# The values of the local attention group read stored parts of h instead of making them from x

## Chip, core and metric

The kernel runs on one core of a Trainium2 chip. The metric is the time of one execution in microseconds on the device. Engines are named as in the profile: PE (TensorE, matrix products), DVE (VectorE), ACT (ScalarE), POOL (GpSimd) and SP (SyncE), which here does nothing but issue DMAs.

## What is computed

One decoder layer over 2048 tokens of width 1024, in float32. A modulated input h feeds one wide projection; three groups of four attention heads with windows of different stride and a gated short convolution follow, are merged, projected, and normalised. Cut to what the change touches:

```
shift, scale, gate = split(silu(c) @ w_ada + b_ada)
h = x * (1 + scale) + shift
q, k, v, g_attn, u, b_gate, c_gate, g_conv, m_attn, m_conv = split(h @ W_in)
for group, (window, dilation) in enumerate(((128, 1), (512, 4), (2048, 16))):
    o[group], lse[group] = dilated_attention(q, k, v of its 4 heads)
o = sum(softmax(lse over groups) * o)
a_out = (o * silu(g_attn)) @ w_attn_out
s_out = (b_gate * conv3(c_gate * u) * silu(g_conv)) @ w_conv_out
y = (sigmoid(m_attn) * a_out + sigmoid(m_conv) * s_out) @ w_o
x = layer_norm(alpha * x + (1 + gate) * y) * ln_g + ln_b
```

## The kernel before

Every matrix product is made of three products of rounded parts: an operand is split into a high part (a cast to fp32r on ACT, L523) and a low part (operand minus high part on DVE, L524), and the products high x high, low x high and high x low are summed in PSUM (L140 to L142, L621 to L623). "Parts" below means such a pair.

**First stage, 0 to about 1540 us: h times W_in.** It runs in two passes p over 1024 tokens each. Of every four blocks of a product, a scheme with seven products instead of eight is used; its stationary or moving operands are sums and differences of the blocks of h. They are the tiles T[1..7, i] (`th`, `tl`), made once per pass for the four rows i by `t_row`. Row i covers k-tile i (tile `xa`) and k-tile i + 4 (tile `xb`), each of 128 rows of h by the 1024 tokens of the pass, that is, two chunks of 512. T[1], T[2] and T[3] are the parts of whole blocks of h: the first chunk of k-tile i, the first chunk of k-tile i + 4, and the second chunk of k-tile i + 4. The second chunk of k-tile i (b12) enters in sums only; no tile holds its parts.
In pass 0 the four rows are made while scale and shift are still being computed: `first_h` loads two w_ada tiles of 512 KB for each k-tile (`wt`, five buffers, L795), forms their dot products with silu(c) on DVE (L720) or by a multiplication on POOL and accumulations on ACT (L724, L727), and then `load_h` loads x (L737, 256 KB each) and turns it into h on ACT (L738). In pass 1 only `load_h` and `t_row` run, interleaved with the last products of pass 0. Tiles `big` (xa, xb and results) have four buffers, half tiles `t` seven.

**Second stage, about 1540 to 2430 us: attention.** Groups 1 and 2 run first. The local group 0 follows, in chunks c of 512 tokens: values V of chunk 0, V of chunk 1, output segments of chunk 0, V of chunk 2, output of chunk 1, V of chunk 3, output of chunks 2 and 3. For V, `prep` loads x for eight k-tiles (`xs`, three buffers, L84), scales and shifts it on DVE (L85) and splits it into `hhi` and `hlo`, rings of 13 tiles that are shared with the rows of the convolution's and the attention's outputs (eight and four tiles per chunk, `prep_rows`, L93). The products of a V are matmuls of 128 columns by 256, `mm<-whi,hhi` and its two companions. Between them stand the merging of the groups (tiles `ab`, `og`, `gt`, `om_scr`) and the gating of outputs (`sg`, L325 and L331).

**Third stage:** the product with W_o and the normalisation.

A scheduler fixes the order of the instructions of each engine when the program is built, and waits are semaphores. Each engine works in its order; all DMAs are issued by SP, in SP's order. An engine reaches an instruction only after the one before it has been issued, and a DMA whose data or buffer is not ready holds up all DMAs behind it.

Of the kernel before, what the change touches and what calls it, by code (L numbers as in the profile page):

```python
# [11 lines left out]
F32 = mybir.dt.float32  # L12
F32R = mybir.dt.float32r
# [4 lines left out]
P = 128  # L18
DM = 1024
SEQ = 2048  # L20
KT = DM // P
CH = 512
# [30 lines left out]


def attention_stage(tc, psum1, wp, hp, kq, pa, pm, split, ident, scp, mod, w_v, w_ao, w_co, xm, xn,
                    qk_scr, nb_scr, ga_scr, o_scr, st_scr, st0_scr, al_scr, om_scr, y_scr, sg_scr, mg_scr):
    nc = tc.nc
    V, S, G, PE, SP = nc.vector, nc.scalar, nc.gpsimd, nc.tensor, nc.sync

# [14 lines left out]
    def parts_of(xs, store):  # L74
        hi = hp.tile([P, CH], F32R, name="hhi", bufs=13)
        lo = hp.tile([P, CH], F32R, name="hlo", bufs=13)
        split(hi, lo, xs)
        store.append((hi, lo))

    def prep(src, store):  # L80
        def pre():
            for k in range(KT):
                xs = hp.tile([P, CH], F32, name="xs", bufs=3)
                SP.dma_start(xs, src[:, k, :])  # L84
                V.tensor_scalar(xs, xs, scp[:, k:k + 1], mod[:, 0, k:k + 1], op0=ALU.mult, op1=ALU.add)  # L85
                parts_of(xs, store)
        return pre

    def prep_rows(srcs, store):
# [315 lines left out]
    for c in range(NCH):  # L405
# [64 lines left out]
        v_prev = heads_of(0, c, h, hb, v_prev, st, done)  # L470
        for jj in range(NH):
            after(len(segs) + 3 + jj // 2, lambda jj=jj, merge=merge: merge(jj))
        pre_all(first, xn[c], h, None)
        if c > 0:
            out_segs(c - 1)
    out_segs(NCH - 1)
# [7 lines left out]
def layer_kernel(ctx: ExitStack, tc: tile.TileContext, x, xm, xn, cvec, wada, bada, w_main, w_v,  # L484
# [25 lines left out]
    nb_scr = dram.tile([3, NH, P, 256], F32, name="nb_scr")  # L510
    qk_scr = dram.tile([24, P, SEQ], F32, name="qk_scr")
    ga_scr = dram.tile([NH, P, SEQ], F32, name="ga_scr")
    o_scr = dram.tile([2, NH, NCH, NCH, P, P], F32, name="o_scr")
    st_scr = dram.tile([2, NCH, NH, 4, 2, NCH, 32], F32, name="st_scr")
    st0_scr = dram.tile([NCH, 2, NH * 4, P], F32, name="st0_scr")
# [40 lines left out]
    def half():  # L556
        return rooms["prep"].tile([P, CH], F32, name="t", bufs=7)
# [4 lines left out]
    def t_split(T, p, i, src):  # L562
        hi = rooms[i].tile([P, CH], F32R, name=f"th{p}{i}")
        lo = rooms[i].tile([P, CH], F32R, name=f"tl{p}{i}")
        split(hi, lo, src)
        T[p, i] = (hi, lo)

    def t_row(T, i, xa, xb):

# [129 lines left out]
    def sum_to(dst):  # L699
        return lambda r, bank: V.tensor_add(dst, r, bank)  # L700

    def t_rows(T, loads):

        def pre():
            for i, load in loads:
                xa, xb = big(), big()
                load(xa, xb)
                t_row(T, i, xa, xb)
        return pre


# [68 lines left out]
    with block_products("s", "prep", (0, 1, 2)) as w:  # L780
# [4 lines left out]
        with tc.tile_pool(name="ada", bufs=1, reuse_waits="tile") as ada:  # L785
# [21 lines left out]
                return load  # L807

            S0 = load_parts(w, w_main[W_Q + NH], w_main[W_Q + NH + 1], CH)
            t_rows(T, [(i, first_h(i)) for i in range(3)])()  # L810
            xa, xb = big(), big()
            first_h(3)(xa, xb)
        open_room((3,))
        t_row(T, 3, xa, xb)
        for n in range(KT):
            SP.dma_start(cw[:, n, :3], convw[n])
        SP.dma_start(cw[:, :, 3], convb)
# [12 lines left out]
        for p in range(2):  # L830
            pre = None
            if p:
                T = {}
                pre = t_rows(T, [(i, load_h(p, i)) for i in range(4)])


            order = [u + g * NH + j for g in (1, 2, 0) for u in (W_Q, W_K) for j in (0, 2)]
# [128 lines left out]
    with ExitStack() as stage:  # L966
        psum1 = stage.enter_context(tc.tile_pool(name="psum", bufs=1, space=bass.MemoryType.PSUM,
                                                 reuse_waits="tile"))
        pool = lambda name: stage.enter_context(tc.tile_pool(name=name, bufs=1, reuse_waits="tile"))
        wp, hp, pm, kq, pa = (pool(n) for n in ("wp", "hp", "pm", "kq", "pa"))  # L970
        attention_stage(tc, psum1, wp, hp, kq, pa, pm, split, ident, scp, mod, w_v, w_ao, w_co, xm, xn,
                        qk_scr, nb_scr, ga_scr, o_scr, st_scr, st0_scr, al_scr, om_scr, y_scr, sg_scr, mg_scr)

    w = ctx.enter_context(block_products("s", (1, 2, 3), (0,), "prep"))

# [119 lines left out]
```

## Time and profile before

| | us |
|---|---|
| median of 3 runs | 2683.31 (2682.05 to 2684.86) |
| profiled execution, its own time | 2677.93 |
| its span, first to last instruction | 2676.1 |
| PE busy | 2468.6 (92%) |
| DVE busy | 1727.0 (65%) |
| ACT busy | 1043.8 (39%) |
| POOL busy | 66.4 (2%) |

The DMA queues moved 361.94 MB; 274.32 MB were read from and 85.51 MB written to HBM. The shares are means over stages with different limits, so they are read by stretches: what counts is where PE is idle, and which engine or queue it waits for there.

### The profile page before, as it was taken

To read this page: it belongs to the slowest core of one execution; us is meant where nothing else is said; L and a number is where in the kernel's file an instruction comes from. 1 tells how busy PE (TensorE), PEld (TensorE's weight loads), DVE (VectorE), ACT (ScalarE), POOL (GpSimd) and SP (SyncE) were. 2 spreads that over 40 slices of the span, in tenths; PEclk is the share of its full clock that TensorE was granted. 3 is DMA by queue.
4 is the path that set the end of the run, shared out by engine and by line. 5 is a ranking of instruction groups with operands and counts; after the bars stand their busy time and mean duration, and the time that the engine had idled before them with its cause. 6 is when DMAs were issued, how large, how long until landed. Compare 5 with 4: busy or idle time off the path is not lost. (4 is left out here: it accounts for less than half of the span.)

```text
span 2676.1 us, 31985 instructions
## 1 busy us (share of the span) xinstructions
PE 2468.6 (92%) x11878; PEld 2091.5 (78%) x11878; DVE 1727.0 (65%) x2867; ACT 1043.8 (39%) x1741; POOL 66.4 (2%) x46
## 2 busy tenths in 40 slices
PE   3999999999999999999999989999998797987884
PEld 2778888888876888888888779999997687864663
DVE  8754566767567555666765355455578777667785
ACT  5323333333344223333333355545563334223443
POOL 2000000000000000000000000000000000000222
PEclk8999999999999999999999989999998898988997
DMA  6334322222343332212122274355558878673332
GB/s 236 119 105 146 107 79 71 68 67 103 126 160 130 104 124 97 87 64 71 63 94 97 87 227 146 110 142 150 161 164 242 268 219 280 202 239 118 126 122 90
DMA packets 196552, 361.94 MB, mean 135 GB/s; under 512 B 21629, under 2 KB 92460, under 8 KB 196396
## 3 DMA queue, kind: packets, MB, share of 16 engines
q1 hardware_dynamic: 196396, 359.90, 42.3%
q8 instruction: 93, 1.52, 0.2%
q14 instruction: 63, 0.52, 0.1%
HBM read 274.32 MB, written 85.51 MB: 134 GB/s over the span
## 5 line engine op out<-in xcount | busy, mean ns | idle before, releaser
L621 PE MATMUL pb<-th,w2h 128*128 128x512 f32 x2016 | 798.4, 397 | 81.3 <-ACT th L523 50.2
L622 PE MATMUL pb<-tl,w2h 128*128 128x512 f32 x2016 | 796.9, 396 | 14.0 <-DVE tl L524 13.9
L623 PE MATMUL pb<-th,w2l 128*128 128x512 f32 x2016 | 793.1, 394 | 5.7 <-DVE w2l L524 5.7
L621 PEld LDWEIGHTS pb<-th,w2h 128*128 128x128 f32 x2016 | 383.3, 190 | 179.8 <-ACT th L523 59.8
L622 PEld LDWEIGHTS pb<-tl,w2h 128*128 128x128 f32 x2016 | 383.6, 190 | 104.3 <-DVE tl L524 25.0
L623 PEld LDWEIGHTS pb<-th,w2l 128*128 128x128 f32 x2016 | 383.8, 190 | 88.3 <-DVE w2l L524 8.8
L524 DVE TENSOR_TENSOR w2l<-raw,w2h 128x1024 fp32r<-128x1024 f32 x168 | 214.1, 1275 | 151.0 <-ACT w2h L523 151.0
L523 ACT CAST w2h<-raw 128x1024 fp32r<-128x1024 f32 x168 | 176.8, 1052 | 287.5 <-PE pb L622 271.6
L630 ACT COPY t<-pb 128x512 f32<-128x512 f32 x248 | 144.6, 584 | 351.7 <-PE pb L623 351.7
L140 PE MATMUL mm<-whi,hhi 128*128 128x256 f32 x768 | 251.5, 328 | 18.8 <-ACT hhi L523 18.6
L142 PE MATMUL mm<-whi,hlo 128*128 128x256 f32 x768 | 248.2, 326 | 2.6 <-DVE hlo L524 2.4
L141 PE MATMUL mm<-wlo,hhi 128*128 128x256 f32 x768 | 248.9, 325 | 0.0
L140 PEld LDWEIGHTS mm<-whi,hhi 128*128 128x128 f32 x768 | 185.7, 242 | 21.4 <-ACT hhi L523 20.9
L142 PEld LDWEIGHTS mm<-whi,hlo 128*128 128x128 f32 x768 | 185.0, 242 | 4.2 <-DVE hlo L524 4.1
L141 PEld LDWEIGHTS mm<-wlo,hhi 128*128 128x128 f32 x768 | 186.2, 242 | 0.0
L140 PE MATMUL mm<-hhi,whi 128*128 128x512 f32 x384 | 155.9, 407 | 30.1 <-DVE sg L331 21.3
L523 ACT CAST whi<-raw 128x1024 fp32r<-128x1024 f32 x96 | 100.7, 1050 | 190.3 <-PE mm L141 87.1
L524 DVE TENSOR_TENSOR wlo<-raw,whi 128x1024 fp32r<-128x1024 f32 x96 | 116.9, 1218 | 68.2 <-ACT whi L523 68.1
L141 PE MATMUL mm<-hlo,whi 128*128 128x512 f32 x384 | 153.6, 400 | 0.7 <-DVE hlo L524 0.7
L142 PE MATMUL mm<-hhi,wlo 128*128 128x512 f32 x384 | 153.5, 400 | 0.0
L523 ACT CAST w2h<-xs 128x1024 fp32r<-128x1024 f32 x84 | 88.6, 1055 | 155.2 <-PE pb L622 127.4
L621 PE MATMUL pb<-th,w1h 128*128 128x512 f32 x336 | 131.8, 392 | 3.3 <-DVE big L1013 2.8
(171 smaller groups left out, 3403.6 us busy)
## 6 DMA issues: line engine op xcount, KB each, us to landing
raw<-in_w_main SPq DMA_DIRECT2D x152, 512.0 KB
qk_scr<-big SPq DMA_DIRECT2D x48, 512.0 KB
raw<-in_w_v SPq DMA_DIRECT2D x48, 512.0 KB
sg_scr<-big SPq DMA_DIRECT2D x32, 512.0 KB
sg<-sg_scr SPq DMA_DIRECT2D x64, 256.0 KB
raw<-in_w_co SPq DMA_DIRECT2D x32, 512.0 KB
qr<-qk_scr SPq DMA_DIRECT2D x48, 256.0 KB
ab<-al_scr SPq DMA_DIRECT2D x48, 256.0 KB
```

Of the source, the lines that this page charges most:

```text
L140: PE.matmul(o, a[0], b[0], start=start, stop=False)
L141: PE.matmul(o, a[0], b[1], start=False, stop=False)
L142: PE.matmul(o, a[1], b[0], start=False, stop=stop)
L523: S.copy(hi, src)
L524: V.tensor_sub(lo, src, hi.bitcast(F32))
L621: PE.matmul(bank, a[0], b[0], start=start, stop=False, **kw)
L622: PE.matmul(bank, a[0], b[1], start=False, stop=False, **kw)
L623: PE.matmul(bank, a[1], b[0], start=False, stop=stop, **kw)
L630: S.copy(r, bank)
```

## The change

A DRAM tensor `h_scr` of 16.8 MB takes the parts of all of h (4 chunks, 8 k-tiles, high and low, 128 x 512 each). In the first stage the rows of T store the pairs that T holds (T[1], T[2], T[3]), and `h_rows` makes and stores the parts of b12: one cast, one subtract, two half tiles. That is eight stores of 256 KB per row, eight rows in all. In the local group `prep_split` loads the high and low parts of a chunk straight into `hhi` and `hlo`: sixteen loads of 256 KB per chunk in place of eight loads of x, eight scalings, eight casts and eight subtracts. Groups 1 and 2 still load and scale x.

```diff
+    def prep_split(c, store):
+        def pre():
+            for k in range(KT):
+                hi = hp.tile([P, CH], F32R, name="hhi", bufs=13)
+                lo = hp.tile([P, CH], F32R, name="hlo", bufs=13)
+                SP.dma_start(hi.bitcast(F32), h_scr[c, k, 0])
+                SP.dma_start(lo.bitcast(F32), h_scr[c, k, 1])
+                store.append((hi, lo))
         return pre
...
-        pre_all(first, xn[c], h, None)
+        segs[first][2] = prep_split(c, h)
...
+    h_scr = dram.tile([NCH, KT, 2, P, CH], F32, name="h_scr")
...
+    def h_out(c, k, pair):
+        for n in range(2):
+            SP.dma_start(h_scr[c, k, n], pair[n].bitcast(F32))
+
+    def h_rows(T, p, i, xa):
+
+        hi, lo = half().bitcast(F32R), half().bitcast(F32R)
+        split(hi, lo, xa[:, CH:PAIR])
+        h_out(2 * p + 1, i, (hi, lo))
...
-    def t_rows(T, loads):
+    def t_rows(T, loads, p=None):
 
         def pre():
             for i, load in loads:
                 xa, xb = big(), big()
                 load(xa, xb)
+                if p is not None:
+                    h_rows(T, p, i, xa)
                 t_row(T, i, xa, xb)
+                if p is not None:
+                    for q, c, k in ((1, 0, i), (2, 0, i + 4), (3, 1, i + 4)):
+                        h_out(2 * p + c, k, T[q, i])
         return pre
...
-            t_rows(T, [(i, first_h(i)) for i in range(3)])()
+            t_rows(T, [(i, first_h(i)) for i in range(3)], 0)()
             xa, xb = big(), big()
             first_h(3)(xa, xb)
         open_room((3,))
+        h_rows(T, 0, 3, xa)
         t_row(T, 3, xa, xb)
+        for q, c, k in ((1, 0, 3), (2, 0, 7), (3, 1, 7)):
+            h_out(c, k, T[q, 3])
...
-                pre = t_rows(T, [(i, load_h(p, i)) for i in range(4)])
+                pre = t_rows(T, [(i, load_h(p, i)) for i in range(4)], p)
```

The change also moves instructions. First place: SP's queue at the start, from the fourth w_ada tile of row 2 on. A name such as `tl_410` is one buffer of a tile; `th_381`, `tl_382` to `th_409`, `tl_410` are T[1], T[2], T[3] of row 2, and `t` is a half tile of `h_rows`. Before, loads of w_ada and x alternate:

```order
L795 DMA wt<-in_wada 128x1024 x4
L737 DMA big<-in_xn 128x512 x4
L795 DMA wt<-in_wada 128x1024 x4
L737 DMA big<-in_xn 128x512 x4
L795 DMA wt<-in_wada 128x1024
L816 DMA cw<-in_convw 128x3 x2
L795 DMA wt<-in_wada 128x1024 x3
L737 DMA big<-in_xn 128x512 x4
L816 DMA cw<-in_convw 128x3 x6
```

Now the stores of a row stand between the loads of the next:

```order
L763 DMA big<-in_xn 128x512 x4
L821 DMA wt<-in_wada 128x1024 x3
L581 DMA h_scr<-t 128x512 x2
L581 DMA h_scr<-th_381 128x512
L581 DMA h_scr<-tl_382 128x512
L581 DMA h_scr<-th_385 128x512
L581 DMA h_scr<-tl_386 128x512
L581 DMA h_scr<-th_409 128x512
L581 DMA h_scr<-tl_410 128x512
L821 DMA wt<-in_wada 128x1024
L763 DMA big<-in_xn 128x512 x4
L845 DMA cw<-in_convw 128x3 x8
```

The last w_ada tile and the four x tiles of row 3 (L821, L763 of the new program) moved from a place behind loads only to a place behind the eight stores of row 2. Second place: SP's queue at the change of pass. Before:

```order
L684 DMA raw<-in_w_main 128x1024 x2
L737 DMA big<-in_xn 128x512 x4
L948 DMA sg_scr<-big 128x1024
L737 DMA big<-in_xn 128x512
L948 DMA sg_scr<-big 128x1024
L737 DMA big<-in_xn 128x512 x11
L684 DMA raw<-in_w_main 128x1024 x3
```

Now, with the stores of row 0 of pass 1 ahead of all but one of the tiles of row 1:

```order
L763 DMA big<-in_xn 128x512 x4
L977 DMA sg_scr<-big 128x1024
L763 DMA big<-in_xn 128x512
L977 DMA sg_scr<-big 128x1024
L581 DMA h_scr<-t 128x512 x2
L581 DMA h_scr<-th_5712 128x512
L581 DMA h_scr<-tl_5713 128x512
L581 DMA h_scr<-th_5716 128x512
L581 DMA h_scr<-tl_5717 128x512
L581 DMA h_scr<-th_5740 128x512
L581 DMA h_scr<-tl_5741 128x512
L763 DMA big<-in_xn 128x512 x6
```

Eleven x loads in a row became six behind eight stores, and the rest further down behind the stores of row 1. Third place: V of chunk 2, first on PE, where `hhi_16772` to `hhi_16793` are the first four k-tiles. Before, from the fourth k-tile on:

```order
L140 MATMUL mm_16879<-whi_16825,hhi_16793 128x256
L141 MATMUL mm_16879<-wlo_16826,hhi_16793 128x256
L142 MATMUL mm_16879<-whi_16825,hlo_16794 128x256
L223 MATMUL pt_17315<-ident_60,p_17236 128x128
L223 MATMUL pt_17315<-ident_60,p_17239 128x128 x2
L223 MATMUL pt_17315<-ident_60,p_17249 128x128
L223 MATMUL pt_17324<-ident_60,p_17249 128x128
L223 MATMUL pt_17324<-ident_60,p_17252 128x128 x2
L223 MATMUL pt_17324<-ident_60,p_17236 128x128
L140 MATMUL s_17335<-kh_17144,qh_17143 128x256
```

Now, at the place of the fourth k-tile and after it (`hhi_16830` is the fourth, `hhi_16846` the eighth):

```order
L150 MATMUL mm_16904<-whi_16850,hhi_16830 128x256
L151 MATMUL mm_16904<-wlo_16851,hhi_16830 128x256
L152 MATMUL mm_16904<-whi_16850,hlo_16831 128x256
L150 MATMUL mm_16904<-whi_16854,hhi_16834 128x256
L151 MATMUL mm_16904<-wlo_16855,hhi_16834 128x256
L152 MATMUL mm_16904<-whi_16854,hlo_16835 128x256
L150 MATMUL mm_16904<-whi_16854,hhi_16838 128x256
L151 MATMUL mm_16904<-wlo_16855,hhi_16838 128x256
L152 MATMUL mm_16904<-whi_16854,hlo_16839 128x256
```

The transposes and scores that stood between k-tile 4 and k-tile 5 are gone from there, and the eight k-tiles follow each other. On SP's queue at the same V, before, from the store of o on:

```order
L465 DMA om_scr<-o_16398 128x512
L65 DMA raw<-in_w_v 128x1024
L333 DMA mg_scr<-sg_16729 128x4x128
L333 DMA mg_scr<-sg_16747 128x4x128
L84 DMA xs<-in_xn 128x512 x3
L320 DMA sg_16833<-sg_scr 128x512
L320 DMA sg_16851<-sg_scr 128x512
L65 DMA raw<-in_w_co 128x1024 x2
L84 DMA xs<-in_xn 128x512
```

Now, with the loads of the parts (L94, L95 of the new program):

```order
L475 DMA om_scr<-o_16447 128x512
L94 DMA hhi<-h_scr 128x512
L65 DMA raw<-in_w_v 128x1024
L343 DMA mg_scr<-sg_16778 128x4x128
L343 DMA mg_scr<-sg_16796 128x4x128
L95 DMA hlo<-h_scr 128x512
L94 DMA hhi<-h_scr 128x512
L95 DMA hlo<-h_scr 128x512
L94 DMA hhi<-h_scr 128x512
L95 DMA hlo<-h_scr 128x512
L94 DMA hhi<-h_scr 128x512
L95 DMA hlo<-h_scr 128x512
```

Three more such pairs follow at once, so that seven pairs stand behind the store of o, and one had been loaded earlier; before, four loads of x stood there, and four had been issued some 40 us earlier.

## Rows read from the trace of the kernel before

**Rows 1.** Page, busy time, share of the span, instructions of TensorE:
```profile
PE 2468.6 (92%) x11878; PEld 2091.5 (78%) x11878; DVE 1727.0 (65%) x2867; ACT 1043.8 (39%) x1741; POOL 66.4 (2%) x46
```

**Rows 2.** Busy time by stretch: us, engines (instructions), clock, DMA share, GB/s:
```profile
0.00:50.00 50.00, 16.16 (x39) 10.13 (x40) 42.08 (x112) 25.10 (x56) 11.16 (x12) 0.93 0.68 239
50.00:100.00 50.00, 40.65 (x146) 29.56 (x145) 46.29 (x94) 26.98 (x48) 4.97 (x2) 0.86 0.45 151
...
800.00:850.00 50.00, 44.57 (x175) 32.60 (x175) 41.17 (x60) 29.56 (x44) 0.00 (x0) 0.97 0.36 121
1900.00:1950.00 50.00, 49.66 (x377) 49.42 (x375) 32.88 (x86) 31.68 (x76) 0.00 (x0) 1.00 0.65 186
...
2100.00:2150.00 50.00, 43.52 (x284) 39.68 (x285) 36.39 (x68) 25.12 (x49) 0.00 (x0) 0.90 0.88 285
...
2200.00:2250.00 50.00, 34.88 (x183) 29.81 (x182) 41.72 (x74) 14.88 (x34) 0.00 (x0) 0.83 0.87 267
```

**Rows 3.** Groups by form, 1900 to 2280, DVE, ACT: busy, mean ns, idle before:
```profile
L524 DVE TENSOR_TENSOR hlo<-xs,hhi 128x512 fp32r<-128x512 f32 x64 | 42.3, 687 | 21.2 <-ACT hhi L523 20.7
L85 DVE TENSOR_SCALAR xs<-xs,scp,mod 128x512 f32<-128x512 f32 x24 | 12.6, 540 | 9.2 <-DMA xs<-in_xn 8.9
...
L523 ACT CAST hhi<-xs 128x512 fp32r<-128x512 f32 x64 | 38.1, 618 | 35.5 <-DVE xs L85 13.0 <-DMA xs<-om_scr 9.9 <-DMA xs<-y_scr 7.1
```

**Rows 4.** Timelines of SP, POOL, ACT, DVE, PE at the start: start, us, instruction:
```profile
47.63 2.54 SPq L795 DMA_DIRECT2D wt<-in_wada  x3
...
51.19 2.57 POOL L724 TENSOR_TENSOR wt<-wt,row 128x1024 f32<-128x1024 f32 x1 [10.33 <-DMA wt<-in_wada]
55.55 2.41 POOL L724 TENSOR_TENSOR wt<-wt,row 128x1024 f32<-128x1024 f32 x1 [1.79 <-DMA wt<-in_wada]
...
67.70 1.24 ACT L738 ACTIVATE big<-big,mod,scp 128x1024 f32<-128x1024 f32 x1 [0.28 <-DVE scp L804]
...
53.98 0.68 DVE L574 TENSOR_TENSOR t<-big 128x512 f32<-128x512 f32 x1
...
55.72 2.78 DVE L524 TENSOR_TENSOR tl<-t,th 128x512 fp32r<-128x512 f32 x1
...
66.53 0.69 DVE L574 TENSOR_TENSOR t<-big 128x512 f32<-128x512 f32 x1
...
74.98 0.69 DVE L524 TENSOR_TENSOR tl<-t,th 128x512 fp32r<-128x512 f32 x1
...
79.41 0.50 PE L621 MATMUL pb<-th,w2h 128*128 128x512 f32 x1 [1.55 <-ACT t L630]
```

**Rows 5.** Timelines of SP, ACT and DVE at the change of pass:
```profile
797.84 13.34 SPq L737 DMA_DIRECT2D big<-in_xn  x11
...
801.58 1.24 ACT L738 ACTIVATE big<-big,mod,scp 128x1024 f32<-128x1024 f32 x1 [0.52 <-DMA big<-in_xn]
...
802.86 0.69 DVE L574 TENSOR_TENSOR t<-big 128x512 f32<-128x512 f32 x1 [0.22 <-ACT big L738]
...
823.74 0.68 DVE L524 TENSOR_TENSOR tl<-big,th 128x512 fp32r<-128x512 f32 x1
```

**Rows 6.** Timelines of SP and PE around the values of chunks 2 and 3:
```profile
2105.39 0.32 SPq L465 DMA_DIRECT2D om_scr<-o  x1
...
2110.93 0.28 PE L140 MATMUL mm<-whi,hhi 128*128 128x256 f32 x1
2111.05 0.28 PE L141 MATMUL mm<-wlo,hhi 128*128 128x256 f32 x1
...
2137.82 0.28 PE L142 MATMUL mm<-whi,hlo 128*128 128x256 f32 x1
...
2237.34 0.58 PE L140 MATMUL mm<-whi,hhi 128*128 128x256 f32 x1 [3.54 <-ACT hhi L523]
```

**Rows 7.** Busy time of the 10 us at V of chunk 2, columns as in 2:
```profile
2110.00:2120.00 10.00, 9.52 (x67) 8.39 (x66) 8.13 (x18) 4.41 (x11) 0.00 (x0) 0.98 0.95 318
```

**Rows 8.** Waits of PE in the whole run: us in total, times, longest:
```profile
PE mm L140 <- DVE sg L331: 21.5, 4, 10.5
```

More of the change, by code (lines that the diff above doesn't have):

```diff
@@ L55, in attention_stage @@
 def attention_stage(tc, psum1, wp, hp, kq, pa, pm, split, ident, scp, mod, w_v, w_ao, w_co, xm, xn,
-                    qk_scr, nb_scr, ga_scr, o_scr, st_scr, st0_scr, al_scr, om_scr, y_scr, sg_scr, mg_scr):
+                    qk_scr, nb_scr, ga_scr, o_scr, st_scr, st0_scr, al_scr, om_scr, y_scr, sg_scr, mg_scr, h_scr):
     nc = tc.nc
@@ L86, in pre @@
                 parts_of(xs, store)
+        return pre
+    def prep_split(c, store):
[6 more added lines that the diff above has]
+                store.append((hi, lo))
         return pre
@@ L971, in layer_kernel @@
         attention_stage(tc, psum1, wp, hp, kq, pa, pm, split, ident, scp, mod, w_v, w_ao, w_co, xm, xn,
-                        qk_scr, nb_scr, ga_scr, o_scr, st_scr, st0_scr, al_scr, om_scr, y_scr, sg_scr, mg_scr)
+                        qk_scr, nb_scr, ga_scr, o_scr, st_scr, st0_scr, al_scr, om_scr, y_scr, sg_scr, mg_scr, h_scr)
     w = ctx.enter_context(block_products("s", (1, 2, 3), (0,), "prep"))
```

## The prediction

> **What bounds the kernel now.** I read the page first: TensorE (PE) is busy 2468.6 us of a span of 2676.1 us [rows 1]. So the time falls only where PE is idle, and it grows wherever PE is made to wait; DVE's 1727 us and ACT's 1044 us cost nothing while PE is fed. Then the table of busy time in 50 us stretches [rows 2]: the reader is to see where the idle lies. The first 100 us leave PE 33.8 + 9.4 = 43.2 us idle, the change of pass at 800 to 850 leaves 5.4 us, the values of chunks 0 and 1 (near 1900 to 1950) run under a full PE (49.66 of 50), and the two stretches with the values of chunks 2 and 3 leave 6.5 and 15.1 us. In all four places with idle PE the vector engine or the DMA engines are near full. The durations of single instructions come from the table of instruction groups [rows 3]. Last I read, inside the four places, the timelines of the engines that PE waits for, to see which queue is last [rows 4 to 6]. The change touches exactly these places, so three terms follow: A start-up, B change of pass, C local attention group.
>
> **A, start-up.** It adds per row i of T one cast on ACT, one subtract on DVE and eight stores of 256 KB on SP's queue. DVE is the busiest engine here (42.1 and 46.3 us of the two 50 us stretches, [rows 2]), so four subtracts of 0.69 us [rows 3] are 2.8 us that nothing hides: the lower bound. A gain is excluded, since nothing is taken away here. The casts (0.62 us) lie beside it on ACT, 25 of 50 us busy.
> The larger part is the queue. Before, SP issued the loads of w_ada and x of the next row as soon as a buffer was free; no load there stands behind work on the row before. Now, by the order shown with the change, the last w_ada tile and the four x tiles of row 3 stand behind the store of a tl split of row 2. SP works in order, so those loads can be issued only when DVE has made that split. Step by step, for row 3: before, its last three w_ada loads were issued from 47.63 us on, within 2.54 us, so the last near 49.8; GpSimd (POOL) multiplied the last at 55.55 for 2.41, the last activation of x (L738) ran at 67.70, the first vector step of row 3 at 66.53, its last split began at 74.98, and PE ran without gaps from 79.41 [rows 4]. After: row 2's first vector step, 53.98 before [rows 4], comes some 1.5 us later by the same queueing one row earlier; the split on which the load hangs is the fifth of its steps, 5 x 0.61 plus one step that took 2.78 in place of 0.69 while POOL multiplied [rows 4] and two dots of 0.4, 6 us: 61.5 to 62. The load is issued then, not at 49.8. Landing takes 3.5 us (47.63 to 51.19) to 5.7 us (49.8 to 55.55) [rows 4]; I take 5, since stores now share the engines: 67. POOL 2.4, four accumulations on ACT 4 x 0.6 = 2.4 and the sum 0.3: 72. Two activations of 1.24, a cast 0.62: about 75.5 to 76 for the first vector step, +9. Thirteen steps of 0.61 end at 83.6, in place of 75.7, +8, and 1.8 us of weight preparation that stood between them before now follows: **A = +10 us**. Upper bound: row 2 slips by one landing too, 5.7 more: +16.
>
> **B, change of pass.** Again 4 x 0.60 = 2.4 us of subtracts on a vector engine that runs back to back up to the last split at 823.74 [rows 5]: lower bound; again nothing is taken away. Before, the eleven last x loads stood behind nothing but free buffers (797.84, 13.3 us for the eleven, [rows 5]). Now three tiles of row 1 and three of row 2 stand behind eight stores of row 0, the last of which waits for a late split of row 0; row 1's first vector step ran at 802.86 before [rows 5], so that split ends no earlier than about 802, and 0.6 later now. A 256 KB load took 3.7 us from issue at 797.84 to the activation at 801.58 [rows 5]; a load issued at 803 feeds an activation at 806.7, and its vector step at 808, in place of 802.86: +5. Row 2's last tile hangs on row 1 in the same way, of which the four buffers hide most, about 1 us. 2.4 + 5 + 1 = **B = +8 us**, upper bound 12 (row 2 pays a whole landing of 3.7 more). PE follows the splits, since it already waits for them here (5.4 us of idle in the stretch).
> The Trainium skill, page "DMA: Bandwidth & Descriptors", section "Anatomy of one DMA — SWDGE (gpsimd) path", fits a DMA as 2.0 us plus bytes over 436 GB/s, for another issuing path; my estimate from it is 2.6 us for 256 KB. The rows above show 3.7 us for such a load in this kernel; by the page's figure the waits in A and B would be some 3 us shorter together, a sum of +21 in place of +24.
>
> **C, local group.** Removed: 32 scalings of 0.54, 32 subtracts of 0.69 (39 us of DVE) and 32 casts of 0.62 (20 us of ACT) [rows 3], and 32 loads. Added: 64 loads of 256 KB, twice the bytes. For chunks 0 and 1 PE is full under them: nothing either way, at most +3 if a pair lands late. For chunk 2: before, V began at 2110.93 and its matmuls, 0.12 us apart, ended at 2137.82 [rows 6] with hardly a wait between, because four tiles were in SBUF early and PE worked on their part, scores and transposes, while the other four came. Now one pair is early and seven, 14 loads or 3.67 MB, stand behind the store of o that was issued at 2105.39 [rows 6], with 1.05 MB more (a weight tile, two stores) among them. PE's new order takes k 0 to 7 one after the other in the first block. The DMA engines are full here, 0.95 busy at 318 GB/s [rows 7]: 4.72 MB take 14.8 us, plus 1.5 to land: 2122. Then 168 of the 192 matmuls are left, 20.2 us: 2142 to 2143, **+5 us**. Behind these loads on SP stand the sg and W_co loads of the next output, wanted only after V. PE has no idle time between V and the next merging, so nothing gives it back there. Chunk 3 has the same queue; it already waits 3.54 us for a cast [rows 6] that is gone, and gets the wait for the pairs: +4. Against this, the vector engine is freed of 16 x 1.23 = 19.7 us in chunks 2 and 3, but most of it lies under full PE or in gaps where DVE itself waited for ab and og tiles from the busy DMA engines; I count 3 us back. **C = +6 us**, bounds -4 (no stall, some relief) and +14 (chunk 1 too, and less hidden).
>
> **Sum.** 10 + 8 + 6 = +24 us. The profiled execution took 2677.93 us, 5.4 below the median of 2683.31; the sum is made on the former, 2702, and carried to the median: **2707 us**. What is done neither at these places nor on SP's queue beside them is unchanged, in its order too.
>
> **Rivals.** (1) *The stores hold up nothing*: their splits are done by the time that SP reaches them, or the loads land before the vector engine gets to them. For it: DVE is full anyway at the start, so a load may be late without harm; against it: 10.33 us of idle on POOL before the tile at 51.19 [rows 4], that is, the chain from w_ada to the activation has no slack at the vector engine's end. Then only the subtracts remain, 2.8 + 2.4, C at 0: +5, 2688 us.
> (2) *Vector relief wins* (faster): PE's idle 21.6 us in 2100 to 2150 and 2200 to 2250 [rows 2] sits next to a vector engine that is 36 to 42 of 50 us busy, and PE's wait there is for the step sg on DVE, 21.5 us in the whole run [rows 8]. If DVE's order there is what counts, all 19.7 us come back and A and B cost 5: -15, 2668 us. It decides once relief exceeds A + B + the stalls; with my A and B it would still be +3. Against it: the DMA engines are 0.88 to 0.95 busy in the same windows and get 8.4 MB more to read.
> (3) *The DMA engines bound the start*: 8.4 MB of stores come into the first 100 us, where the share is 0.45 to 0.68 at 151 to 239 GB/s [rows 2]. If they add wholly, 8.4 MB at 280 GB/s, halfway between 239 and 318, are 30 us: A = +30, sum +44, 2727 us. Against it: a third to a half of the engines' time is free.
>
> **Chances and range.** A measurement of this kernel can tell about 0.2%, 5.4 us, from no change. Forecast 0.73; rival 1: 0.11; rival 2: 0.09; rival 3: 0.07. Faster 0.09, same 0.11 (rival 1), slower 0.80. The forecast's terms at their lower and upper ends are 2.8 + 2.4 - 4 = +1 and 16 + 12 + 14 = +42; all three at one end at once is unlikely, so the range goes from rival 1's edge, 2685, to 2725, and leaves out rival 2, the far end of rival 3 and little of the forecast.
>
> **What would show it.** A right: the last w_ada load of row 3 near 62 us on SP, behind a store; POOL's last multiplication near 67; PE gap-free from about 89; PE busy in 50 to 100 near 31 in place of 40.65. A wrong: the loads at their old times, or PE gap-free by 83. B right: the last split of pass 1 near 832, PE idle in 800 to 850 near 13 in place of 5.4. C right: PE waits for a DMA into hhi or hlo of some 10 us near 2112, and V of chunk 2 ends some 5 us later after A + B are taken off; the waits on sg remain. C wrong: V waits under 2 us and the idle in 2200 to 2250 falls well below 15: then the relief was worth more than I gave it. The forecast as a whole falls if the stores wait for nothing on SP.

## The result

| | us |
|---|---|
| before, median of 4 runs | 2682.68 (2678.18 to 2684.86) |
| after, median of 4 runs | 2716.31 (2714.31 to 2718.14) |
| ratio, 95% interval | 1.0132 (1.012 to 1.0145) |
| span of the profiled execution, before and after | 2676.1 and 2714.9 |

The change makes the kernel 33.6 us slower. The forecast was +24, to 2707; the range reached 2725. The two profiled executions lie 38.8 us apart, 5.2 more than the medians: that of before (2677.93) was 4.75 us under its median, that of after (2716.72) 0.4 over. Where the terms are read from the two traces, they add up to 38.8.

The page of after, first row as in [rows 1]:

```profile
PE 2488.3 (92%) x11878; PEld 2106.0 (78%) x11878; DVE 1696.6 (62%) x2811; ACT 1031.6 (38%) x1717; POOL 65.5 (2%) x46
```

DVE has 30 us less to do and ACT 12, as the change intends; PE is busy 20 us more with the same 11878 matmuls, so part of them ran at the lower clock. The stretches of [rows 2] in after (us, busy time of PE, PE's weight loads, DVE, ACT and POOL with their instructions, granted clock, DMA share, GB/s):

```profile
0.00:50.00 50.00, 18.33 (x42) 11.50 (x42) 41.42 (x113) 23.53 (x44) 8.49 (x11) 0.97 0.80 282
50.00:100.00 50.00, 26.86 (x80) 19.04 (x81) 36.12 (x83) 24.88 (x58) 7.03 (x3) 0.73 0.68 233
800.00:850.00 50.00, 36.09 (x110) 25.33 (x110) 33.84 (x54) 31.38 (x44) 0.00 (x0) 0.74 0.78 274
...
2100.00:2150.00 50.00, 31.81 (x136) 25.05 (x134) 32.84 (x50) 8.83 (x16) 0.00 (x0) 0.84 0.92 258
2150.00:2200.00 50.00, 49.66 (x305) 45.12 (x306) 29.85 (x59) 20.86 (x40) 0.00 (x0) 0.88 0.88 281
```

The second 50 us have 26.9 us of PE in place of 40.7, the change of pass 36.1 in place of 44.6, and DVE is now *less* busy in both (36.1 for 46.3, 33.8 for 41.2): it waits for data that it did not wait for before. The granted clock of the last row is 0.88 with PE full.

**Delay at the same instruction.** The traces hold the same stores, so one can subtract the time of the same store in before. A is read at the first store of q and k, B at the 31st less the 24th, C from there to the last store of the output. The last row is the end of the span, which in the runs where POOL issues DMAs comes later after that store (see POOL loads):

| place (us in before) | after | stage 1 only | loads only | no casts | late stores | pass 0 only | pass 1 only | row 3 late | POOL loads | late, POOL | POOL pass 1 | pass 1, POOL | gated |
|---|---|---|---|---|---|---|---|---|---|---|---|---|---|
| 1st q/k store, 86.27 | 14.7 | 16.3 | -1.7 | 15.9 | 2.5 | 15.6 | -0.1 | 12.2 | 15.8 | 1.5 | 2.4 | -0.2 | 1.6 |
| 24th q/k store, 299.92 | 16.0 | 17.5 | 1.5 | 17.2 | 3.8 | 16.3 | 0.2 | 13.6 | 16.5 | 2.2 | 3.8 | 0.2 | 2.8 |
| 31st q/k store, 884.61 | 28.3 | 29.9 | 1.9 | 29.0 | 9.0 | 17.0 | 11.8 | 26.2 | 28.2 | 9.5 | 14.8 | 10.8 | 8.2 |
| o of group 2, 1916.14 | 27.3 | 29.2 | 2.3 | 29.7 | 6.7 | 16.4 | 11.6 | 25.0 | 28.4 | 8.5 | 15.2 | 10.2 | 8.1 |
| last o of chunk 1, 2105.39 | 32.1 | 31.3 | 2.6 | 34.2 | 15.9 | 21.7 | 9.8 | 29.9 | 35.2 | 15.4 | 23.2 | 18.9 | 13.6 |
| first o of chunk 2, 2203.01 | 39.5 | 31.0 | 9.0 | 41.9 | 21.5 | 24.4 | 16.7 | 36.2 | 30.6 | 9.1 | 17.7 | 13.6 | 8.1 |
| last output, 2672.64 | 38.8 | 29.7 | 10.5 | 43.0 | 25.6 | 21.1 | 17.7 | 35.9 | 29.7 | 7.3 | 15.2 | 10.3 | 4.7 |
| end of the span, 2676.1 | 38.8 | 29.7 | 10.5 | 43.0 | 25.6 | 21.1 | 17.7 | 35.9 | 32.3 | 9.9 | 20.4 | 12.9 | 11.2 |

For the change: A 14.7 (and 1.3 more between the first and the 24th store, where PE waits for small tiles as before but the granted clock fell further after it), B 12.3, C 10.5. One execution stands behind each column, and single places move by 1 to 2 us between executions.

**A in the trace of after**, timelines of SP, POOL, DVE, ACT and PE (start, us, engine, line, instruction, idle time before it), to be held against [rows 4]:

```profile
63.80 0.63 SPq L821 DMA_DIRECT2D wt<-in_wada  x1
...
69.82 2.34 POOL L750 TENSOR_TENSOR wt<-wt,row 128x1024 f32<-128x1024 f32 x1 [10.40 <-DVE scp L830]
...
76.69 0.69 DVE L535 TENSOR_TENSOR t<-big,t 128x512 fp32r<-128x512 f32 x1 [2.42 <-ACT t L534]
...
83.85 0.69 DVE L535 TENSOR_TENSOR tl<-t,th 128x512 fp32r<-128x512 f32 x1
...
82.04 1.78 SPq L705 DMA_DIRECT2D raw<-in_w_main  x3
...
87.35 1.04 ACT L534 CAST w2h<-raw 128x1024 fp32r<-128x1024 f32 x1 [3.53 <-DMA raw<-in_w_main]
...
88.43 1.22 DVE L535 TENSOR_TENSOR w2l<-raw,w2h 128x1024 fp32r<-128x1024 f32 x1 [3.88 <-ACT w2h L534]
...
94.12 0.50 PE L642 MATMUL pb<-th,w2h 128*128 128x512 f32 x1 [0.29 <-ACT t L651]
```

The last w_ada tile of row 3 is issued at 63.8 behind the stores of row 2, the multiplication runs at 69.8, row 3's first vector step at 76.7, its last split begins at 83.9. Then come two rows that the prediction had not: three weight tiles of W_in, issued at 82.0 behind the stores of row 3, and the cast that waits 3.5 us for them, with DVE behind it for 3.9. PE runs without gaps from 94.1, before from 79.4.

**B in the trace of after**, SP, ACT and DVE, to be held against [rows 5], and the busy time of one stretch:

```profile
811.49 1.24 ACT L764 ACTIVATE big<-big,mod,scp 128x1024 f32<-128x1024 f32 x1
...
813.58 0.60 ACT L534 CAST t<-big 128x512 fp32r<-128x512 f32 x1
...
814.21 0.69 DVE L535 TENSOR_TENSOR t<-big,t 128x512 fp32r<-128x512 f32 x1 [1.90 <-ACT t L534]
...
819.76 3.25 SPq L763 DMA_DIRECT2D big<-in_xn  x6
...
824.49 1.24 ACT L764 ACTIVATE big<-big,mod,scp 128x1024 f32<-128x1024 f32 x1 [3.52 <-DMA big<-in_xn]
...
826.41 0.69 DVE L535 TENSOR_TENSOR t<-big,t 128x512 fp32r<-128x512 f32 x1 [4.72 <-ACT t L534]
...
844.88 0.69 DVE L535 TENSOR_TENSOR t<-big,t 128x512 fp32r<-128x512 f32 x1 [3.57 <-ACT t L534]
```

```profile
820.00:830.00 10.00, 6.12 (x13) 4.14 (x14) 5.11 (x9) 6.09 (x9) 0.00 (x0) 0.50 0.84 293
```

DVE stands idle for 4.7 us before row 1 and for 3.6 us before row 3, both times for x tiles that were issued behind stores; its first step of the pass, at 814.21, is the subtract of b12, which comes up under *What is left of the change of pass*. PE, short of parts, works at the lower clock (0.50, the 1.2 GHz level).

**C in the trace of after**, SP and PE at V of chunk 2, to be held against [rows 6], and PE's wait near the values of chunk 1 with what came late on ACT:

```profile
2137.47 0.32 SPq L475 DMA_DIRECT2D om_scr<-o  x1
...
2150.64 0.32 SPq L95 DMA_DIRECT2D hlo<-h_scr  x1
...
2142.53 0.28 PE L150 MATMUL mm<-whi,hhi 128*128 128x256 f32 x1
...
2147.96 0.58 PE L152 MATMUL mm<-whi,hlo 128*128 128x256 f32 x1 [4.12 <-DMA hlo<-h_scr]
...
2161.28 0.41 PE L152 MATMUL mm<-whi,hlo 128*128 128x256 f32 x1
2161.49 0.32 PE L150 MATMUL mm<-whi,hhi 128*128 128x256 f32 x1
...
1977.05 0.63 ACT L185 ACTIVATE qh<-qr 128x512 fp32r<-128x512 f32 x1 [3.36 <-DMA qr<-qk_scr]
...
1982.80 0.90 PE L233 MATMUL pt<-ident,p 128*128 128x128 f32 x3 [6.08 <-DVE rows L361]
```

V starts with one pair and a half, waits 4.1 us for the second pair's low part, then goes at the pace of the loads to 2156 and at the lower clock to 2161 (matmuls 0.21 apart, 0.12 before). The o of chunk 2 is 7.4 us later against before than the o of chunk 1. Between 1945 and 2020 another 4.8 us are lost, for which the prediction had put 0 to 3: one part of it is a q tile, queued among the loads of parts for chunk 1, that lands late: ACT waits for it, and DVE and PE behind ACT. The same wait of PE was 4.13 us before, so this is 2.0 of the 4.8; where the rest goes I have not traced.

### The profile page after: what moved, and what is told of

Same layout as the page of the kernel before. It is cut to its first block, busy times and chain, and to the rows that moved or that the text cites. A ratio compares the mean times of both kernels' runs of the same rounds, so it can differ in the third digit from the quotient of the medians.

```text
span 2714.9 us, 32070 instructions
## 1 busy us (share of the span) xinstructions
PE 2488.3 (92%) x11878; PEld 2106.0 (78%) x11878; DVE 1696.6 (62%) x2811; ACT 1031.6 (38%) x1717; POOL 65.5 (2%) x46
## 5 line engine op out<-in xcount | busy, mean ns | idle before, releaser
L150 PE MATMUL mm<-whi,hhi 128*128 128x256 f32 x768 | 253.9, 331 | 16.6 <-ACT hhi L534 13.8
L152 PEld LDWEIGHTS mm<-whi,hlo 128*128 128x128 f32 x768 | 186.3, 243 | 10.6 <-DMA hlo<-h_scr 7.0
```

What stands on the lines that cost most here:

```text
L150: PE.matmul(o, a[0], b[0], start=start, stop=False)
L152: PE.matmul(o, a[1], b[0], start=False, stop=stop)
```

## The experiments

My theory: the stores cost by their place on SP's queue, ahead of loads that something waits for; the loads of parts likewise. Rivals: the bytes cost wherever they stand, since the DMA engines are full; the added casts and subtracts cost, since DVE is full. Each kernel is built on the change or on another run; the times stand beside runs of the kernel before on the same chip.

| run | median us | before | ratio, 95% interval | span |
|---|---|---|---|---|
| stage 1 only | 2706.46 | 2679.3 | 1.0099 (1.0084 to 1.0114) | 2705.8 |
| loads only | 2689.32 | 2679.3 | 1.0045 (1.0029 to 1.0061) | 2686.7 |
| no casts | 2719.55 | 2679.3 | 1.0149 (1.0134 to 1.0164) | 2719.1 |
| late stores | 2696.68 | 2679.3 | 1.0069 (1.0053 to 1.0084) | 2701.8 |
| pass 0 only | 2699.19 | 2679.16 | 1.008 (1.0065 to 1.0095) | 2697.2 |
| pass 1 only | 2695.17 | 2679.16 | 1.0058 (1.0041 to 1.0075) | 2693.9 |
| POOL loads | 2710.02 | 2679.16 | 1.0117 (1.0102 to 1.0132) | 2708.4 |
| late stores, POOL loads | 2689.05 | 2679.16 | 1.0044 (1.0029 to 1.006) | 2686.0 |
| row 3 late | 2717.47 | 2681.69 | 1.0134 (1.0121 to 1.0148) | 2712.1 |
| late, POOL in pass 1 | 2699.66 | 2681.69 | 1.0075 (1.0059 to 1.009) | 2696.5 |
| pass 1 only, all by POOL | 2693.67 | 2681.69 | 1.0047 (1.0034 to 1.006) | 2689.0 |
| gated stores | 2692.99 | 2675.02 | 1.0067 (1.0053 to 1.008) | 2687.4 |

### One half of the change at a time

Stage 1 only:

```diff
-        segs[first][2] = prep_split(c, h)
+        pre_all(first, xn[c], h, None)
```

> The first stage is the changed one (casts, subtracts, all 64 stores); the local group makes its parts from x as before, so nothing reads the stored parts. Queue theory (loads of the next row wait on SP behind the stores of this row): the whole delay of the first stage stays and the local group costs nothing, so a span of 2676.1 + 14.7 (start) + 1.3 + 12.3 (change of pass) = about 2704, and a time some 27 us above the kernel before. If the cost of the change lay in the local group, the time would be within 5 us of before.

Measured: +27.2 us (2706.46 against 2679.3), and the columns of the table follow those of after up to 1916. The first stage alone costs some four fifths of the change.

Loads only:

```diff
-                SP.dma_start(hi.bitcast(F32), h_scr[c, k, 0])
-                SP.dma_start(lo.bitcast(F32), h_scr[c, k, 1])
+                SP.dma_start(hi.bitcast(F32), h_scr[0, k, 0])
+                SP.dma_start(lo.bitcast(F32), h_scr[0, k, 1])
...
+                    if p == 0 and u == order[3]:
+                        for i in range(4):
+                            h_out(0, i, T[1, i])
+                            h_out(0, i + 4, T[2, i])
```

> The local group loads 64 tiles of parts as in the change, but always those of chunk 0, which are stored from T[1] and T[2] of pass 0 late in the first stage, behind the first weights; no parts of b12 are made and nothing is stored at the change of pass, so the values of chunks 1 to 3 are those of chunk 0. Theory: start and change of pass as before (0 to +1 us), the local group the measured +11 to +13: span 2687 to 2690. Rival (vector relief helps once the first stage is left alone): the span falls below 2676.

Measured: +10.0 us, the span 2686.7; 6.3 us of it come at V of chunk 2. The local group costs time with DVE 32 us less busy (1694.6 in place of 1727.0), even where the first stage is left alone. Rival 2 of the prediction (vector relief wins) falls for the loads as the change places them.

### Casts or stores

```diff
-                    h_rows(T, p, i, xa)
...
-                    for q, c, k in ((1, 0, i), (2, 0, i + 4), (3, 1, i + 4)):
+                    for q, c, k in ((1, 1, i), (1, 0, i), (2, 0, i + 4), (3, 1, i + 4)):
```

> All 64 stores stay at their places behind the splits, but the parts of b12 are not made (eight times one cast and one subtract per pass row are left out); the parts of T[1] are stored in their place, so these values are wrong. Queue theory: nearly all of the delay stays, less at most 2.8 + 2.4 us: span 2709 to 2715. Rival (the added casts and subtracts on full engines are the cost): the first stage returns to the old times, span about 2688.

Measured: nothing comes back, the span is 2719.1, 4 above the change; A is 15.9 and B 11.8. So the added vector work is no cost on top of the stores, which now stand behind a split of T[1]. That it would cost nothing without them is not shown. At the change of pass the first vector step is on time again, at 794.9 with the delay so far taken off, but DVE then waits 6.8 us before row 1, where it waited 4.7 in after, for loads issued at the same place:

```profile
826.68 0.69 DVE L595 TENSOR_TENSOR t<-big 128x512 f32<-128x512 f32 x1 [6.83 <-ACT big L764]
```

### The same stores later

```diff
+    late, soon = [], []
+
+    def h_out(c, k, pair, todo=late):
+        def out_():
+            for n in range(2):
+                SP.dma_start(h_scr[c, k, n], pair[n].bitcast(F32))
+        todo.append(out_)
...
-        h_out(2 * p + 1, i, (hi, lo))
+        h_out(2 * p + 1, i, (hi, lo), soon)
...
                 load(xa, xb)
+                flush_out(soon)
...
                     step(w, w_main[u], w_main[u + 1], CH, use, pre)
                     pre = None
+                    flush_out(soon)
+                    if u == order[3]:
+                        flush_out(late)
```

> Same work and the same 64 stores, but issued later: the stores of the b12 parts of a row stand behind the loads of the next row, and those of T[1] to T[3] behind the first weights of the pass. Queue theory: start costs about 3 to 4 us in place of 14.7, change of pass 3 to 5 in place of 12.3, local group unchanged at 12: span 2694 to 2698. Rival (the bytes themselves crowd the DMA engines): the stores still fall into the same 40 us and the start stays near +15, span above 2708.

Measured: A falls from 14.7 to 2.5, B from 12.3 to 5.2, and the time from +33.6 to +17.4. The span, 2701.8, is above what I expected, because this execution lost more than the change's in the local group (16.6 after the 31st store, 10.5 in after); by the median the local group cost about 8 (17.4 less 3.8 and 5.2). SP, and PE's last gap, in this run:

```profile
44.17 7.12 SPq L830 DMA_DIRECT2D wt<-in_wada  x4
51.39 1.80 SPq L772 DMA_DIRECT2D big<-in_xn  x4
...
61.68 1.11 SPq L713 DMA_DIRECT2D raw<-in_w_main  x2
...
81.93 0.50 PE L650 MATMUL pb<-th,w2h 128*128 128x512 f32 x1 [1.62 <-ACT t L659]
```

The w_ada tiles of row 3 are issued by 51.3 and the first weights at 61.7; PE runs without gaps from 81.9. In the first 100 us the same casts are made and nearly as many bytes move (263 and 246 GB/s in the two halves, 282 and 233 in after), so at the start it is the place in the queue that costs, and rival 3 falls there.

### Half of the tokens

```diff
-        segs[first][2] = prep_split(c, h)
+        if c < 2:
+            segs[first][2] = prep_split(c, h)
+        else:
+            pre_all(first, xn[c], h, None)
...
-                pre = t_rows(T, [(i, load_h(p, i)) for i in range(4)], p)
+                pre = t_rows(T, [(i, load_h(p, i)) for i in range(4)])
```

> Only pass 0 makes and stores parts, and only chunks 0 and 1 load them; chunks 2 and 3 make theirs from x as before. If the terms stand for themselves: start +14.7 to +16, change of pass 0, some 2 to 5 us where the values of chunks 0 and 1 load (a qr tile lands later), no step of 7 us at the values of chunk 2: span 2692 to 2697. If the loads of chunks 0 and 1 cost nothing under the full PE, as the prediction had it, 2691 to 2692.

Measured: span 2697.2, +20.0 us; 5.3 us are lost between the o of group 2 and the last o of chunk 1, 2.6 at the next place. The expectation's upper value held: the loads of chunks 0 and 1 are not free. What they cost scatters: by the first o of chunk 1 the runs that load parts on SP lost 2.6 to 7.5 us since the o of group 2, the two without any loads of parts there 0.7 and 1.8.

The other half (`c >= 2`, with pass 0 as in the kernel before):

> Only pass 1 makes and stores parts, and only chunks 2 and 3 load them. Start 0, change of pass +12.3, +6 to +7 at the values of chunk 2 (seven pairs behind the store of o) and +1 to +3 at chunk 3: span 2695 to 2699. If the delay at chunk 2 only came from the delay before it, the span is 2689.

Measured: span 2693.9, a little under what was expected; A -0.1, B 11.6, 6.9 us at V of chunk 2 with no delay ahead of it. C of the two halves is 21.1 - 17.0 = 4.1 and 17.7 - 11.8 = 5.9, together 10.0; the change has 10.5. The terms stand for themselves.

### The missing step at the start

```diff
-        for q, c, k in ((1, 0, 3), (2, 0, 7), (3, 1, 7)):
-            h_out(c, k, T[q, 3])
...
+                    if p == 0 and u == order[3]:
+                        for q, c, k in ((1, 0, 3), (2, 0, 7), (3, 1, 7)):
+                            h_out(c, k, T[q, 3])
```

> The change, with one move: the six stores of T[1] to T[3] of row 3 of pass 0 stand behind the next three loads of weights, not ahead of them; the two stores of the b12 parts stay ahead. If the part of the start that the prediction missed (weights loaded at 82.0 in place of 58.2 us) is this queueing, the first store of results comes 3 to 5 us earlier than in the changed kernel (at 96 to 98 in place of 101.0) and the span is 2709 to 2712. If row 3's splits alone set the start, nothing moves: 2713 to 2716.

Measured: the weights are issued at 79.39 in place of 82.04, the first store comes at 98.43, 2.6 us earlier than in after: the step is there, and smaller than I expected. Its cast waits 0.7 us for the weights in place of 3.5:

```profile
84.18 1.05 ACT L534 CAST w2h<-raw 128x1024 fp32r<-128x1024 f32 x1 [0.71 <-DMA raw<-in_w_main]
```

Part of the rest is that row 3 itself began 0.9 us later in this execution, at 77.56. In the times (1.0134 against 1.0132) it can't be told.

### The loads of parts on another queue

```diff
-                SP.dma_start(hi.bitcast(F32), h_scr[c, k, 0])
-                SP.dma_start(lo.bitcast(F32), h_scr[c, k, 1])
+                G.dma_start(hi.bitcast(F32), h_scr[c, k, 0])
+                G.dma_start(lo.bitcast(F32), h_scr[c, k, 1])
```

> The change, with the 64 loads of parts issued by POOL, which is idle in this stage, in place of SP: they wait for free ring slots alone and for no store ahead of them. Queue theory for the local group: the stall of PE at the values of chunk 2 goes and most of the 7 us there with it, span 2704 to 2710. Rival (the DMA engines are full, so the bytes come no sooner): the same 11 to 13 us in the local group, span 2713 to 2718.

Measured: the span falls to 2708.4, as the queue theory had it, and the 7.4 us at V of chunk 2 turn into a gain of 4.6. But the merging ahead of it now loses 7 to 8 us that it did not lose before. POOL, the busy time of 10 us, DVE and PE in this run:

```profile
2100.93 0.54 POOL L95 DMA_DIRECT2D hlo<-h_scr  x1 [84.61 <-PE mm L152]
```

```profile
2110.00:2120.00 10.00, 1.06 (x5) 0.56 (x3) 1.01 (x2) 0.00 (x0) 2.01 (x4) 0.66 1.01 365
```

```profile
2118.99 2.04 DVE L470 TENSOR_TENSOR ab<-ab,og 128x512 f32<-128x512 f32 x2 [9.93 <-DMA ab<-al_scr]
...
2123.55 0.77 PE L150 MATMUL mm<-hhi,whi 128*128 128x512 f32 x1 [12.49 <-DVE sg L335]
```

Some 3.7 MB of parts start at 2101, as soon as slots are free; the DMA engines are wholly busy at 365 GB/s, DVE waits 9.9 us for an ab tile of the merging, and PE 12.5 us. The bytes have to pass somewhere: the queue only chooses who waits. The Trainium skill says so in "DMA: Bandwidth & Descriptors", section "Issuing engines are not separate DMA queues": transfers started by different engines share the same 16 DMA engines. These rows agree.

A second cost of this queue comes after the last store: POOL's closing instruction, which the span contains, is longer the more DMAs POOL has issued. Before (none), in the next run (64, as here), in POOL pass 1 (96) and in gated (112), shortest, median and longest in ns:

```profile
L1091 POOLq DRAIN  x3: 34/78/2439, 2670.2 to 2675.9; - x3
L1133 POOLq DRAIN  x3: 40/93/7694, 2677.5 to 2685.8; - x3
L1136 POOLq DRAIN  x3: 40/102/10307, 2685.4 to 2696.2; - x3
L1139 POOLq DRAIN  x3: 40/102/11616, 2675.0 to 2687.1; - x3
```

It grows by 0.082 us for each DMA, and the span ends 2.6, 5.2 and 6.5 us later after the last store than in before. So in the runs with POOL the last two rows of the table differ.

Late stores and loads by POOL together:

> Late stores in the first stage (as in the run with late stores) and the loads of parts issued by POOL. If both are matters of the queue: start +2.5 to 3.8, change of pass +5, local group +3 to +6: span 2687 to 2692. It beats the kernel before only if the vector relief is worth more than the queue shows, that is with a local group of -10 or better, which I do not expect. Rival (bytes): 2694 or more.

Measured: +9.9 us, span 2686.0: A 1.5, B 7.3, C -2.2, and 2.6 us of POOL's closing instruction. It is the cheapest form of the whole change that I found, and still slower than before.

### What is left of the change of pass

On top of the last run, the 32 stores of pass 1 are issued by POOL at once:

```diff
+                (SP if c < 2 else G).dma_start(h_scr[c, k, n], pair[n].bitcast(F32))
```

> As the run with late stores and loads by POOL, and the 32 stores of pass 1 are issued by POOL too, so that SP's x loads at the change of pass have the order of before. Queue theory: the change of pass costs the four subtracts and little more, 2.4 to 4 us in place of 7.3; start +2, local group -2 to 0: span 2679 to 2682. If the bytes of the stores beside the x loads are what is left, the change of pass stays at 6 to 8 us: span 2683 to 2687.

Measured: the expectation was wrong by the whole term. SP's order is that of before, and B rises to 11.0:

```profile
802.32 18.77 SPq L775 DMA_DIRECT2D big<-in_xn  x11
...
812.12 1.24 ACT L776 ACTIVATE big<-big,mod,scp 128x1024 f32<-128x1024 f32 x1 [2.62 <-DMA big<-in_xn]
```

```profile
810.00:820.00 10.00, 7.27 (x24) 4.92 (x22) 6.50 (x11) 7.33 (x11) 3.76 (x7) 0.83 1.03 381
```

The eleven x loads take 18.8 us in place of 13.3 [rows 5], with DMA engines wholly busy at 381 GB/s. Here the bytes beside the loads cost nearly as much as the place behind them did. Of its +18.0 us 5.2 are POOL's closing instruction. Another run has only pass 1, with stores and loads by POOL (the `c >= 2` kernel with `G` in both places):

> Only chunks 2 and 3 use stored parts; the stores of pass 1 and the loads are all issued by POOL. Start 0; change of pass 2.4 to 4 by the queue theory, 6 to 8 if the bytes count; local group between -4 and 0, since the vector engine loses 16 scalings and 16 subtracts around the merging. Queue theory: span 2675 to 2680, the same as before within 0.2%. It would have to come below 2671 to beat the kernel before.

Measured: the time is 2693.67, B 10.6, C -0.4. It confirms B, and shows that chunks 2 and 3, where DVE is busiest, gain nothing that can be told; 2.6 us more are POOL's closing instruction.

Last, the 24 stores of T of pass 1 held back until row 3 is made, each behind a store of 64 bytes of row 3's tl into the same place:

```diff
+                if gate is not None:
+                    G.dma_start(h_scr[c, k, n][0:1, 0:16], gate[0:1, 0:16].bitcast(F32))
...
+                    if p == 1:
+                        while late:
+                            late.pop(0)(T[3, 3][1])
```

> As the run with late stores and loads by POOL, but the 24 stores of T[1] to T[3] of pass 1 are held back until row 3's last parts exist: POOL issues them, each behind a store of 64 bytes of row 3's tl into the same place, so no x load of the pass has them ahead of it, on a queue or in the DMA engines. The eight stores of b12 parts stay behind the next row's loads. If stores ahead of the x loads are what the change of pass costs, by queue or by bytes, it now costs 2.4 to 4 us in place of 7.3 (and 11 with immediate stores by POOL): span 2679 to 2683. If it stays at 7 or more, what is left is the subtracts and casts, or the order of the weights behind, and the span is 2685 to 2689.

Measured: B is 5.4, between the two expectations. Now the DMA engines have room while row 3 is made and DVE hardly waits:

```profile
820.00:830.00 10.00, 7.68 (x27) 4.61 (x26) 9.03 (x16) 8.45 (x14) 2.21 (x5) 0.97 0.25 90
```

So of the 12.3 us of B, about 7 are the stores, by queue or by bytes. The other 5.4, nearly the 5.2 of late stores, fit the split of b12. Its four subtracts are 2.4 us by their count; 3.3 more come from its place, first in the row. The first vector step of the pass needs only the scaled xa before, and runs 0.04 us after it:

```profile
793.60 1.24 ACT L738 ACTIVATE big<-big,mod,scp 128x1024 f32<-128x1024 f32 x1 [0.30 <-DMA big<-in_xn]
...
794.88 0.69 DVE L574 TENSOR_TENSOR t<-big 128x512 f32<-128x512 f32 x1
```

In after it is the subtract of b12 at 814.21, which waits for its cast, and this cast stands on ACT behind the scaling of xb (811.49). With the 16.0 us of delay taken off, that is 798.2, 3.3 us later. The ten runs that make b12 in pass 1 are 3.0 to 3.8 us late at this step, the three that don't 0.0 to 0.2. No run moves the split behind the other steps of its row, so what that would give back stays open.

The last store of this execution is only 4.7 us late (C -3.5), yet its span ends 11.2 us later, because POOL's closing instruction takes 6.5 more. Its median lies 18.0 us above the kernel before on that chip (2675.02): this execution ran 3.9 us under its own median, and that chip's before 2.9 under the profiled one. Whether it is better than the run without the gate is not settled.

## Why the prediction came out as it did

**What bounds the kernel** held: most of the time went to the four places where PE had idle time. Outside them went the 4.8 us around the values of chunk 1, where the prediction had PE full, and 1.3 us near 190 us, where PE waits for small tiles as before (1.1 and 2.3 us, now 1.3 and 2.1) and the granted clock was then 0.80 in place of 0.90. That the time lies inside the range owes something to the range: its top stood 18 us above the forecast, and A, B and C were each too small, by 4.7, 4.3 and 4.5.

**A, forecast +10, measured 14.7.** The chain was right in its order: issue 62 forecast, 63.8 measured; multiplication 67 and 69.8; first vector step 75.5 to 76 and 76.7; end of the last split 83.6 and 84.5. Two errors in it nearly cancelled, which is luck: row 2's first vector step came at 58.69 and not at 55.5, and the load was issued 5.1 us after it and not 6 to 6.5. The failed step is the last, "1.8 us of weight preparation that stood between them before now follows". I costed the vector steps of that preparation and not the loads behind them: the three W_in tiles stand behind row 3's stores on the same queue, issued at 82.0 where they had been issued at 58.2, so the preparation began with 3.5 us of waiting on ACT and 3.9 on DVE. The end of the last split came 8.9 us later than before, the preparation added its 1.8 and this wait 3.9, together 14.6. The row 3 run shows the step, with 2.6 us of it back. Every queue entry behind the stores had to be looked at, not the next row's alone.

**B, forecast +8, measured 12.3,** a little over its upper bound of 12. DVE's wait for row 1 is the forecast's 5 us (4.7). The signs came near: last split at 853.3, or 837.3 with the delay taken off (832 forecast), PE idle 13.9 us (13). The term "Row 2's last tile hangs on row 1, of which the four buffers hide most, about 1 us" held for row 2, where ACT waited 0.95 us; put at nothing was the same for row 3, whose x tiles were issued at 835.9 and 838.6 behind stores of row 2 (3.6 us). Put at nothing too was the place of the split of b12: I charged two activations and a cast before the first step of a row at the start, and not here, where they make it 3.3 us late. And the queue is not the only cause: in the POOL pass 1 run it is clear and the wait is there all the same, since 8.4 MB of stores share the DMA engines with the x loads. Over the 5.4 us of the split, the bytes beside the loads cost 5.6 there, the place ahead of them 6.9 in after. (The no casts run, B 11.8 without the split, shows that split and stores don't simply add.)

I argued that case, as rival 3, for the start only, where the late stores show it not to hold; the place where it holds is the change of pass. For the load in question I took 3.7 us from the row of before; the first of the six tiles behind the stores took 4.7 us to its activation. The Trainium skill's fit ("DMA: Bandwidth & Descriptors", "Anatomy of one DMA — SWDGE (gpsimd) path"), by which my estimate for 256 KB was 2.6 us, is made for DMAs that GpSimd issues. In POOL loads these took 3.1 to 10.8 us from issue to landing, 6.5 in the median, so the trace, with the DMA engines busy, does not agree with it here.

**C, forecast +6, measured 10.5.** Chunk 2: +5 forecast, 7.4 measured, by the mechanism described. For the forecast's 1.5 us of landing after the transfer no run has a row; the second pair's low part took 5.7 us from its place in the queue (2142.3) to its matmul. PE waited 4.1 us and not 10 at a time, then went at the pace of the loads and afterwards at the lower clock, which the forecast had not charged. Chunks 0 and 1: 0 forecast, "at most +3 if a pair lands late", 4.8 measured. The step that failed is the sentence "for chunks 0 and 1 PE is full under them: nothing either way": a q tile behind the pairs came late, which is 2.0 of the 4.8; PE had waited 4.13 us at the same place before, so it was not full there. The rest is not traced. Chunk 3 and relief: +4 and -3 forecast; from the first o of chunk 2 to the last output, -0.7 measured.

**Rivals.** (1), the stores hold up nothing, fell with the first comparison of SP's rows. (2), vector relief wins, fell in size: with the loads moved to POOL, C is between +1.5 and -3.5 in five traces, where 19.7 us were at stake, and with POOL's closing instruction between +0.4 and +5.6. In POOL loads, DVE's freed time lies where it waits 9.9 us for an ab tile. (3) fell at the start and came true, in small, at the change of pass. No variant was faster than the kernel before.

## What to carry to other kernels

On an in-order queue a store that waits for a result holds up every load behind it, so a new store is costed by going through all that stands behind it up to where the queue runs dry, weights included; here it was cheapest behind the last load that anyone waits for. Work put first in a row is costed by what it waits for, not by its own length. Moving a DMA to an idle engine's queue helps only if the DMA engines have room at that moment: look at their share in that stretch first, and at the issuing engine's end of the program. And trading vector work for twice the bytes gained little here, at most 3.5 of 19.7 us net of the loads, in a stretch where the vector engine itself waits for DMAs.

## What the runs showed of the hardware

- Loads and stores together moved 381 GB/s in one 10 us stretch (share 1.03) and 365 in another. That is no gain over loads alone, which reached 405 in before:

```profile
6.00:16.00 10.00, 0.00 (x0) 0.00 (x0) 8.34 (x12) 3.88 (x5) 0.00 (x0) 1.00 1.02 405
```

- A DMA of 256 KB that POOL issues keeps POOL for 0.54 us, and each DMA that it has issued makes its closing instruction 0.082 us longer (2.44 us with none, 7.69, 10.31 and 11.62 with 64, 96 and 112).
- A short wait costs more than itself. PE waited 4.1 us at V of chunk 2 of after; the granted clock was 0.50 (the 1.2 GHz level) from 2148 to 2161.5, with PE busy 5.50 of the last 5.50 us, and 1.00 (2.4 GHz) from there. Some 25 matmuls of 128 by 256 columns, after the loads had landed, came 0.21 us apart in place of 0.12: about 2.3 us more than the wait itself.
